# An estimate of engine times that orders a two-layer encoder program: its costs and slacks are changed

## The chip, the cores and the metric

The kernel runs on one core of one Trainium2 chip. The metric is the device time of one execution in microseconds; lower is better. The median of three executions before the change is 1813.26 us (1812.84 to 1814.89).

## The reference

A trunk of two residual layers over 512 tokens of width 1024, all in float32. Each layer adds half a gated feed-forward block, a mixer, and half a second feed-forward block to the residual stream; every part works on the root-mean-square norm of the stream:

```python
def _swiglu(h, w_gate, w_up, w_down):
    return (jax.nn.silu(h @ w_gate) * (h @ w_up)) @ w_down      # 1024 -> 2816 -> 1024

for layer in range(2):
    x = x + 0.5 * _swiglu(_rmsnorm(x, ...), ...)
    h = _rmsnorm(x, mix_norm[layer])
    if layer == 0:   # SSD heads (Mamba-2, chunks of 64) beside an S5 mixer (complex diagonal, 32 groups of 64 states)
        mixed = concat(ssd(h @ w[:, a]), s5(h @ w[:, b])) @ even_w_out
    else:            # chunked band attention beside a pooling mixer of four windows
        mixed = concat(attention(...), pool(...)) @ odd_w_out
    x = x + mixed
    x = x + 0.5 * _swiglu(_rmsnorm(x, ...), ...)
```

The S5 mixer needs tables that depend on its parameters only (powers of the discretised state matrix, input and output gains of 8 steps). The kernel works them out on the chip.

## The kernel before

**Stages.** Six stages run one after the other: f0 (first feed-forward), even (SSD and S5), f1, f2, odd (attention and pooling), f3. The residual stream lies transposed in eight tiles x of 128x512. A weight tile is loaded as float32 (raw, 512 KB), and split into a rounded part, copied by ScalarE (ACT), and a rest, taken by VectorE (DVE), both in tile whl. A product is then three matmuls (high by high, high by low, low by high), each 128x512, accumulated in a bank of PSUM (tile ps). Most of each feed-forward stage works on 256 columns with a scheme that needs seven block products for eight ("pairs"); the first tiles of it are done in the plain way ("classical"). In f0 the plain way reaches to q = 9 of 11, since the S5 tables are prepared beside it.

**Order.** Each engine runs its instructions in program order, and that order comes from a small simulation in the builder. `Builder` walks the main matmuls in a fixed order; after every group of three it calls `tick`, which moves on a set of generators ("threads", sorted by `PRIO`): the feed of split weights, evacuations of PSUM (`evac`), gates, norms, S5 and SSD pieces, attention blocks and the preparation of the S5 tables (`s5_prepare`). A generator says what it needs with `yield from self.on(engine, tiles)`, and goes on when the estimate says that this is there. `Clock` keeps the estimate: a time for each engine, and for each 64 elements of each tile the time of the last write and read. `Clock.cost` gives an instruction's duration, `Clock.note` moves the times. "Now" is the estimated time of TensorE (PE). So the estimate costs nothing at run time; it decides only which instruction stands ahead of which in each engine's order. What the chip waits for are semaphores that follow from the data.

**What `on` asks.** For PE a thread goes on when its inputs were ready `SLACK[stage]` before now (1.5 us in f0, 0.0 in even, 0.4 in odd). For ACT and DVE it goes on when inputs are ready within 0.3 us and the engine's estimated backlog is under `BACKLOG[stage]` (2.5 us in f0 and even, 3.0 in odd). With `ps=1` it also asks `side` for a bank of PSUM.

**Banks.** Eight banks lie in two pools of four, "b" for projection tiles, "a" for the down projections. `side` lets side work have a bank of "b" while fewer than `sideb` (2) are open, and else one of "a"; a bank counts as free from the estimated time of its last reader. `side_ps` asks `side` again and takes the bank.

**Table products.** In `s5_prepare`, `gains_of_outputs(e)` (eight times, two in flight) makes g1 on DVE, multiplies it by bmx in eight matmuls on PE (in the profile ps<-g,s5bm), copies the result to kt on ACT and writes it to HBM (prm). `gains_of_inputs(e)` (eight times, one in flight) makes bt on DVE, transposes it on PE (ps<-ident,bt), copies it to bl and writes it. The stage even reads prm.

**S5 in even.** `s5_bounce` writes u to HBM (s5us) and reads it back in 16 DMAs with runs of 64 elements into tile hg; `s5_eighth` multiplies that with the tables.

All compute instructions go through `Engine.call`, so nearly every row of the profile has its line, L205; tiles tell the rows apart.

Of the kernel before, what the change touches and what calls it, by code (L numbers as in the profile page):

```python
# [8 lines left out]
F32 = mybir.dt.float32  # L9
# [5 lines left out]
PSUM = bass.MemoryType.PSUM  # L15
DRAM = bass.MemoryType.DRAM

P = 128
S = 512
# [13 lines left out]
for _i, _pools in enumerate(((),(3,),(2,),(1,0))):  # L33
# [19 lines left out]
LAG = 4  # L53
WARM = 12
SLACK = {"f0": 1.5, "even": 0.0, "f1": 0.0, "f2": 0.0, "odd": 0.4, "f3": 0.0}
PRIO = {"evac": 0, "gate": 0, "small": 5, "prep": 6, "blocks": 6, "s5_bounce": 1, "s5_quarter": 0, "s5_gate": 0, "s5_eighth": 1,
        "ssd_dt": 1, "conv": 1, "ssd_chunk": 1, "ssd_tail": 0, "z": 2, "qk_norm": 0, "pool": 3, "attn": 2}
LIVE = 3
# [50 lines left out]
class Clock:  # L109


    def __init__(self):
        self.t = dict.fromkeys(list(ENGINES.values()) + ["RING", "DMA"], 0.0)
        self.t["ACT"], self.t["RING"], self.t["DVE"], self.t["PE"] = 1.9, 0.65, 0.6, 0.95
        self.w, self.r, self.floor, self.stuck = {}, {}, 0.0, 0
        self.lanes, self.born = [0.0] * 8, {}

    @property
    def now(self):
# [22 lines left out]
    @staticmethod  # L142
    def cost(eng, op, out, kw):
        n = max(out.free_size(), kw["in_"].free_size() if op == "tensor_reduce" else 0)
        if eng == "PE":
            if op == "transpose":
                return 0.12
            if kw["lhsT"].dtype == F32R:
                return max(0.11, 0.0025 + n / 2400)
            if out.partition_size() == 64:  # L150
                return 0.035 + n * 0.00084
            return max(0.21, 0.04 + n * 0.00168) if n < 512 else 0.86
        if eng == "ACT":
            return (0.2 if hasattr(kw.get("scale"), "space") or hasattr(kw.get("bias"), "space") else 0.09) + n * 0.00084
        one = op in ("tensor_scalar", "tensor_copy") and kw.get("in0", kw.get("in_")).space != PSUM
        ptr = any(hasattr(kw.get(k), "space") for k in ("scalar", "scalar1"))
        return (0.128 if ptr else 0.068) + n / (1920 if one else 960) * (1 if eng == "DVE" else 2)

    def note(self, eng, op, args, kw):
        out = kw.get("out", args[0] if args else None)  # L160
        outs = [out] + ([kw["accum_out"]] if "accum_out" in kw else [])
        ins = [v for k, v in kw.items() if k not in ("out", "accum_out") and hasattr(v, "free_size")]
        dma = op == "dma_start"
        at = self.t["RING"] if dma else self.t[eng]
        for ap in ins:
            for b in self.blocks(ap):
                t, e = self.w.get(b, (0.0, ""))
                at = max(at, t + (0.15 if e != eng else 0.11 if eng != "PE" else 0.0))
        for ap in outs:
            at = max(at, self.born.get(ap.name, 0.0))  # L170
            for b in self.blocks(ap):
                t, e = self.w.get(b, (0.0, ""))
                at = max(at, 0.0 if dma and e == "DMA" else t if e == eng else t + 0.1, self.r.get(b, 0.0))
        if dma and eng == "POOL":
            self.t["POOL"] = max(at, self.t["POOL"]) + 1.1
            end = max(self.t["DMA"], self.t["POOL"] + 1.0) + max(0.18, out.free_size() * out.partition_size() * 4 / 360e3)
            self.t["DMA"] = end
            end += 0.95
        elif dma:
            at = max(at, self.lanes.pop(0))  # L180
            self.t["RING"] = at + 0.48
            end = max(self.t["DMA"], at + 1.1) + max(0.06, out.free_size() * out.partition_size() * 4 / 360e3)
            self.t["DMA"] = end
            end += 1.06
            self.lanes.append(end)
        else:
            end = at + self.cost(eng, op, out, kw)
            self.t[eng] = end
        for ap in outs:
            for b in self.blocks(ap):  # L190
                self.w[b] = (max(end, self.w.get(b, (0.0, ""))[0]), "DMA" if dma else eng)
        for ap in ins:
            for b in self.blocks(ap):
                self.r[b] = max(self.r.get(b, 0.0), end)
# [55 lines left out]
class Builder:  # L250
# [44 lines left out]

    def add(self, kind, gen):
        p = PRIO[kind]
        i = next((i for i, (q, _) in enumerate(self.threads) if q >= p), len(self.threads))
        self.threads.insert(i, (p, gen))

    def idle(self):
# [13 lines left out]
            self.idle()  # L315


    def on(self, eng, *aps, ps=0):
        c = self.clk
        while True:  # L320
            r = c.ready(*aps)
            if eng == "PE":
                ok = r + SLACK[self.name] <= c.now
            elif eng == "DMA":
                ok = r <= c.now + 0.5
            else:
                ok = r <= c.now + 0.3 and c.t[eng] <= c.now + self.backlog
            if ok and (not ps or self.side(ps) is not None):
                return
            yield  # L330

# [22 lines left out]
            self.ring_of.pop(t.name).give(t)  # L354


    def side(self, n=1):
        which = None
        for w, most in (("b", self.sideb), ("a", 4)):
            ok = min(most - self.open[w], sum(t <= self.clk.now for t in self.freed[w]))  # L360
            if ok > 0:
                which = w
                n -= ok
        return which if n <= 0 else None
# [473 lines left out]
    def evac(self, ps, t, tag, m, done):  # L838
        while not self.scaled():
            yield  # L840
        if t[tag] is None:
            yield from self.room(tag, 1)
            if t[tag] is None:
                t[tag] = self.ft.tile([P, 2, S], F32, tag=tag, name=self.n(tag), bufs=1)
            else:
                self.leave(tag)
        yield from self.on("DVE", ps, self.rsB)
        self.evac_rs(ps, t[tag][:, m])
        self.free(ps)
        done.append(1)  # L850
# [84 lines left out]
    def pair(self, w, tag):  # L935
# [11 lines left out]
        self.nc.scalar.copy(out=p1, in_=X[:, hi])  # L947
        dst = self.ftile(tag)
        add(dst[:, 0, lo], X[:, lo], p1)
        self.free(X)  # L950
        Y = self.main_ps()
        a = self.block(Y[:, lo], W3, 0, TA, lo)
        self.block(Y[:, hi], W3, 512, TA, hi, a)
        self.give(W3)
        add(u2, Y[:, hi], p1)
        add(dst[:, 0, hi], Y[:, lo], u2)
        Z = self.main_ps()
        a = self.block(Z[:, lo], W4, 512, N[4:8], hi)
# [86 lines left out]
    def s5_prepare(self, pool):  # L1045
# [57 lines left out]
        for j in range(8):  # L1103
            n = 7 - j
# [26 lines left out]
        bmx, t16, t17 = tl("s5bm", [G + 1, 16]), tl("s5t16", [G, 16]), tl("s5t17", [G, 16])  # L1131
# [29 lines left out]
        def gains_of_outputs(e):  # L1161
# [3 lines left out]
            g1 = pool.tile([P, 4, 9, 16], F32, tag="s5g1", bufs=2, name=self.n("g1"))  # L1165
# [8 lines left out]
            nc.sync.dma_start(out=part(1), in_=g1[:, :, 1:9].rearrange("p g j i -> p g (j i)"))  # L1174
            yield from self.on("DVE")

            yield from self.on("PE", g1, bmx, ps=1)
            psk = self.side_ps()
            for i in range(4):
                nc.tensor.matmul(out=psk[32 * i:32 * i + 32, 0:P],  # L1180
# [20 lines left out]
        def gains_of_inputs(e):  # L1201
            gs = slice(4 * e, 4 * e + 4)
            prm = self.prm[e]
            part = lambda n: prm[:, 512 * n:512 * n + 512].rearrange("p (g c) -> p g c", g=4)
            bt = pool.tile([P, 4, 8, 16], F32, tag="s5bt", name=self.n("bt"))
            sh = [P, 4, 8, 16]
            v.tensor_tensor(out=bt, in0=brr[:, gs].unsqueeze(2).to_broadcast(sh),
                            in1=x1[:, gs].unsqueeze(3).to_broadcast(sh), op=ALU.mult)
            tb = pool.tile([P, 4, 8, 16], F32, tag="s5tc", name=self.n("tc"))
            v.tensor_tensor(out=tb, in0=bri[:, gs].unsqueeze(2).to_broadcast(sh),  # L1210
                            in1=x2[:, gs].unsqueeze(3).to_broadcast(sh), op=ALU.mult)
            v.tensor_tensor(out=bt, in0=bt, in1=tb, op=ALU.add)
            yield from self.on("PE", bt, ps=1)
            pst = self.side_ps()
            for i in range(4):
                nc.tensor.transpose(out=pst[:, i * P:(i + 1) * P], in_=bt[:, i].rearrange("p j i -> p (j i)"),
                                    identity=self.ident)
            bcal = pool.tile([P, 512], F32, tag="s5bl", bufs=2, name=self.n("bl"))
            yield from self.on("ACT", pst)
            nc.scalar.copy(out=bcal, in_=pst)  # L1220
            self.free(pst)
            yield from self.on("DMA", bcal)
            nc.sync.dma_start(out=prm[:, 0:512], in_=bcal)
            yield from self.on("DVE")
# [866 lines left out]
```

## Time and profile before

| | |
|---|---|
| median of three executions | 1813.26 us |
| the profiled execution | 1810.71 us, span 1808.7 us from first to last instruction |
| PE busy | 1792.4 us (99% of the span), 10514 matmuls |
| PE weight loads | 1564.3 us (86%) |
| DVE busy | 1428.9 us (79%), 2599 instructions |
| ACT busy | 754.7 us (42%), 1082 instructions |
| DMA | 207.16 MB, mean 115 GB/s |
| granted TensorE clock | 0.999 of full speed |

Busy time of PE counts a matmul up to its modelled end, and matmuls overlap; a distance between the starts of two matmuls says more of its rate than the busy time. Idle time of other engines costs nothing while PE has work. In rows of the timeline the first number is the start, the second the length, both in us; the bracket is the idle time ahead of it and what ended it.

### The profile page before, as it was taken

What the parts mean: (1) busy time and instruction counts of PE and PEld (TensorE: products, weight loads), DVE (VectorE), ACT (ScalarE), POOL (GpSimd) and SP (SyncE); (2) the same over time, 40 slices, a digit from 0 to 9 for tenths busy, and PEclk for the clock granted to TensorE, in tenths of its full rate; (3) what the DMA queues carried; (4) which work ended last, traced back from release to release, by engine and by line L of the source; (5) the groups of instructions that cost most, each with busy time, mean ns of one, the idle gap of its engine ahead of it and who ended that gap; (6) DMA issues with size and microseconds to landing.
All of it is one profiled execution on the core that took longest, in us unless ns stands there. A gap on an engine that the chain in (4) does not pass through costs nothing.

```text
span 1808.7 us, 26795 instructions
## 1 busy us (share of the span) xinstructions
PE 1792.4 (99%) x10514; PEld 1564.3 (86%) x10514; DVE 1428.9 (79%) x2599; ACT 754.7 (42%) x1082; POOL 18.7 (1%) x35
## 2 busy tenths in 40 slices
PE   9999999999999999999999999999999999999999
PEld 7877888978878889999988999998888788999997
DVE  8989877878986878887777988775578678988864
ACT  4323423433574444343343444333466544434331
POOL 0000000000010000000000000000000000000000
PEclk9999999999999999999999999999999999999999
DMA  5247432337773223332422333332434422333331
GB/s 196 92 141 190 144 103 82 117 130 205 201 168 114 88 89 104 118 105 95 138 64 78 106 117 97 103 102 86 144 78 111 129 82 76 100 106 107 111 98 70
DMA packets 80749, 207.16 MB, mean 115 GB/s; under 512 B 18000, under 2 KB 30320, under 8 KB 79472
## 3 DMA queue, kind: packets, MB, share of 16 engines
q1 hardware_dynamic: 78032, 196.52, 34.6%
q0 software_dynamic: 2448, 8.91, 3.1%
q8 instruction: 83, 1.36, 0.3%
q14 instruction: 42, 0.34, 0.1%
q10 hardware_dynamic: 144, 0.02, 0.0%
HBM read 192.82 MB, written 12.60 MB: 114 GB/s over the span
## 4 chain that ended last, share of the span: by engine, by line
PE 88%; DVE 8%; DMA 2%; issue 1%; ACT 1%; SPq 0%; DVEq 0%; ACTq 0%
PE ps L205 88%; DVE whl L205 1%; DVE hg L205 1%; DVE us L205 1%; DVE ex L205 1%; DVE ssb L205 1%; DMA raw<-in_wglu_dram 0%; DMA prm<-prm 0%; DMA s5ys<-ys 0%; ACT whl L205 0%; DVE s5x L205 0%; DMA ssb<-acsd 0%; DVE sc L205 0%; ACT hg L205 0%; DMA raw<-in_wgu_dram 0%
## 5 line engine op out<-in xcount | busy, mean ns | idle before, releaser
L205 PE MATMUL ps<-hg,whl 128*128 128x512 f32 (+1 forms) x8688 | 1609.6, 345 | 5.5 <-DVE hg L205 2.5
L205 PEld LDWEIGHTS ps<-hg,whl 128*128 128x128 f32 x8688 | 1375.5, 190 | 203.8 <-issue 4.6
L205 ACT CAST whl<-raw 128x1024 fp32r<-128x1024 f32 x366 | 383.0, 1051 | 532.3 <-PE ps L205 323.4
L205 DVE TENSOR_TENSOR whl<-raw,whl 128x1024 fp32r<-128x1024 f32 x349 | 424.1, 1222 | 180.8 <-ACT whl L205 180.3
L205 DVE SCALAR_TENSOR_TENSOR x<-ps,x 128x512 f32<-128x512 f32 x128 | 87.1, 688 | 37.0 <-PE ps L205 35.4
L205 DVE TENSOR_TENSOR raw<-raw,raw 128x512 f32<-128x512 f32 (+1 forms) x182 | 111.3, 649 | 2.2
L205 ACT CAST hg<-us 128x512 fp32r<-128x512 f32 x88 | 52.1, 620 | 105.2 <-DVE us L205 104.9
L205 PE MATMUL ps<-hg,wh 128*128 128x256 f32 x624 | 83.4, 283 | 0.0
L205 ACT ACTIVATE gs<-gs 128x1024 f32<-128x1024 f32 x44 | 46.7, 1060 | 85.5 <-DVE gs L205 85.5
L205 PEld LDWEIGHTS ps<-hg,wh 128*128 128x128 f32 x624 | 78.6, 192 | 0.0
L205 DVE TENSOR_TENSOR raw<-raw 128x512 f32<-128x512 f32 (+1 forms) x78 | 46.6, 597 | 16.4 <-DMA raw<-in_wgu_dram 16.4
L205 ACT COPY p<-ps 128x256 f32<-128x256 f32 x52 | 19.3, 372 | 95.5 <-PE ps L205 86.1
L205 DVE TENSOR_TENSOR hg<-us,hg 128x512 fp32r<-128x512 f32 x88 | 57.9, 685 | 0.0
L205 DVE TENSOR_TENSOR us<-gs,us 128x1024 f32<-128x1024 f32 x44 | 53.6, 1219 | 0.4
L205 ACT ACTIVATE hg<-x,gains 128x512 fp32r<-128x512 f32 x48 | 33.6, 722 | 32.4 <-DVE x L205 30.0
L205 ACT CAST hg<-raw 128x512 fp32r<-128x512 f32 x58 | 34.4, 622 | 21.3 <-DVE raw L205 20.6
L205 DVE TENSOR_TENSOR hg<-raw,hg 128x512 fp32r<-128x512 f32 x58 | 38.1, 689 | 0.1
L205 DVE SCALAR_TENSOR_TENSOR hg<-x,gains,hg 128x512 fp32r<-128x512 f32 x48 | 34.9, 746 | 2.5 <-ACT hg L205 2.5
L205 DVE TENSOR_TENSOR wh<-raw,wh 128x512 fp32r<-128x512 f32 x52 | 35.7, 686 | 0.0
L205 DVE TENSOR_TENSOR us<-ps,rsB 128x512 f32<-128x512 f32 x40 | 28.9, 723 | 4.5 <-PE ps L205 4.4
L205 ACT CAST wh<-raw 128x512 fp32r<-128x512 f32 x52 | 32.0, 616 | 0.0
L205 DVE TENSOR_TENSOR acc<-acc,sq 128x512 f32<-128x512 f32 x42 | 29.0, 690 | 0.9
(264 smaller groups left out, 1100.0 us busy)
## 6 DMA issues: line engine op xcount, KB each, us to landing
raw<-in_wgu_dram SPq DMA_DIRECT2D x176, 512.0 KB, 3.6
raw<-in_wdn_dram SPq DMA_DIRECT2D x88, 512.0 KB, 3.6
raw<-in_wev_dram SPq DMA_DIRECT2D x16, 512.0 KB, 3.6
prm<-prm SPq DMA_DIRECT2D x8, 1024.0 KB, 6.9
raw<-in_wod_dram SPq DMA_DIRECT2D x12, 512.0 KB, 3.6
raw<-in_wevo_dram SPq DMA_DIRECT2D x8, 512.0 KB, 6.6
raw<-in_wodo_dram SPq DMA_DIRECT2D x8, 512.0 KB, 6.4
x<-in_xT_dram SPq DMA_DIRECT2D x8, 256.0 KB, 5.6
```

Of the source, the lines that this page charges most:

```text
L205: r = f(*args, **kw)
```

## The change

It changes costs in `Clock`, the order of equal threads, and the slack of two places; no instruction is added or removed by it, other than what follows from another order.

- `Clock.cost`: a split matmul takes (n + 32) / 2400 us instead of max(0.11, 0.0025 + n / 2400): 0.2267 instead of 0.2158 for 512 columns, 0.120 instead of 0.110 for 256. A reciprocal takes 0.07 + n x 0.0062.
- `Clock.moved`: a DVE instruction takes 0.09 us more where its first partition, in quarters of 32, differs from that of the last read or write in the same memory.
- `Clock.short`: a DMA whose contiguous runs are under 128 elements, with at least 256 runs, lands 2.0 us later. By the shapes these are the 16 reads of s5us alone.
- `add`: an evac goes behind the threads of its priority, no longer ahead of them.
- `evac` reserves its tile in another way.
- `side` takes a slack: a bank must have been free that long. `on` hands its slack to it.
- The two kinds of table products ask for `PREP_SLACK` (3.0 us) instead of 1.5.

```diff
+PREP_SLACK = 3.0
...
+        self.reads, self.writes = {}, {}
...
             if kw["lhsT"].dtype == F32R:
-                return max(0.11, 0.0025 + n / 2400)
+                return (n + 32) / 2400
...
+        if op == "reciprocal":
+            return 0.07 + n * 0.0062
         return (0.128 if ptr else 0.068) + n / (1920 if one else 960) * (1 if eng == "DVE" else 2)
+
+    def moved(self, ins, out):
+        at = lambda ap: (ap.space == PSUM, ap.start_partition() // 32)
+        held = any(self.reads.get(m, q) != q for m, q in map(at, ins))
+        m, q = at(out)
+        held = held or self.writes.get(m, q) != q
+        self.writes[m] = q
+        for m, q in map(at, ins[::-1]):
+            self.reads[m] = q
+        return 0.09 if held else 0.0
+
+    @staticmethod
+    def short(aps):
+        def run(ap):
+            n = 1
+            for st, m in list(ap.ap)[:0:-1]:
+                if st != n:
+                    break
+                n *= m
+            return n
+        r = min(map(run, aps))
+        return 2.0 if r < 128 and aps[0].free_size() * aps[0].partition_size() >= 256 * r else 0.0
...
-            end += 1.06
+            end += 1.06 + self.short([out] + ins)
...
             end = at + self.cost(eng, op, out, kw)
+            if eng == "DVE":
+                end += self.moved([ap for ap in ins if ap.free_size() > 1], out)
...
     def add(self, kind, gen):
         p = PRIO[kind]
-        i = next((i for i, (q, _) in enumerate(self.threads) if q >= p), len(self.threads))
+        i = next((i for i, (q, _) in enumerate(self.threads) if q > p or q == p and kind != "evac"), len(self.threads))
...
-    def on(self, eng, *aps, ps=0):
+    def on(self, eng, *aps, ps=0, slack=None):
         c = self.clk
+        slack = SLACK[self.name] if slack is None else slack
...
-                ok = r + SLACK[self.name] <= c.now
+                ok = r + slack <= c.now
...
-            if ok and (not ps or self.side(ps) is not None):
+            if ok and (not ps or self.side(ps, slack) is not None):
...
-    def side(self, n=1):
+    def side(self, n=1, slack=0.0):
...
-            ok = min(most - self.open[w], sum(t <= self.clk.now for t in self.freed[w]))
+            ok = min(most - self.open[w], sum(t + slack <= self.clk.now for t in self.freed[w]))
...
     def evac(self, ps, t, tag, m, done):
         while not self.scaled():
             yield
+        while t[tag] is None and self.cnt.get(tag, 0):
+            yield
         if t[tag] is None:
-            yield from self.room(tag, 1)
-            if t[tag] is None:
-                t[tag] = self.ft.tile([P, 2, S], F32, tag=tag, name=self.n(tag), bufs=1)
-            else:
-                self.leave(tag)
+            self.cnt[tag] = 1
+            t[tag] = self.ft.tile([P, 2, S], F32, tag=tag, name=self.n(tag), bufs=1)
...
-            yield from self.on("PE", g1, bmx, ps=1)
+            yield from self.on("PE", g1, bmx, ps=1, slack=PREP_SLACK)
...
-            yield from self.on("PE", bt, ps=1)
+            yield from self.on("PE", bt, ps=1, slack=PREP_SLACK)
```

## The prediction, as put on record

> **What bounds the kernel now.** I read the page first (busy shares and the chain that ended last), then stretches, then who PE waited for, then the worst wait in the timeline.
>
> ```profile
> span 1808.7 us, 26795 instructions
> PE 1792.4 (99%) x10514; PEld 1564.3 (86%) x10514; DVE 1428.9 (79%) x2599; ACT 754.7 (42%) x1082; POOL 18.7 (1%) x35
> PE 88%; DVE 8%; DMA 2%; issue 1%; ACT 1%; SPq 0%; DVEq 0%; ACTq 0%
> ```
>
> PE is busy for all but 16.3 us of the span, and 88% of the chain is PE. The change adds and removes no matmul, so what it can win is PE's idle time and matmuls that ran slowly. The next rows say in which stages that lies, and the list of waits what it is (engine and tile that waited, what for, total, times, longest).
>
> ```profile
> 20.00:100.00 80.00, 78.36 (x361) 64.53 (x360) 76.23 (x266) 23.57 (x31) 0.00 (x0) 1.00 0.32 99
> 600.00:700.00 100.00, 100.00 (x596) 89.52 (x595) 88.18 (x136) 46.30 (x62) 0.00 (x0) 1.00 0.27 91
> ...
> PE ps L205 <- DVE hg L205: 3.0, 3, 1.5
> PE ps L205 <- DVE us L205: 2.9, 1, 2.9
> PE ps L205 <- DVE ones L205: 1.1, 1, 1.1
> PE ps L205 <- DVE whl L205: 1.1, 2, 0.5
> PE ps L205 <- DMA hg<-s5us: 0.8, 1, 0.8
> ...
> PE ps L205 <- DVE cr L205: 0.2, 1, 0.2
> ```
>
> The stretches are: length, then busy us of PE, PEld, DVE, ACT and POOL with their counts, granted clock, DMA share, GB/s. From 600 to 700 us, inside a later feed-forward stage, PE is busy 100.00 of 100: such stretches have nothing to win. The eleven rows of waits (first five and the last are shown) sum to 11.6 us in 14 waits. 2.7 us of that are at the start (ones, whl twice by DVE and 0.5 by ACT). The largest single one is 2.9 us, a table product in f0:
>
> ```profile
> 97.40 0.96 PE L205 MATMUL ps<-hg,whl 128*128 128x512 f32 x3
> 101.22 0.42 PE L205 MATMUL ps<-g,s5bm 128*32 128x128 f32 x8 [2.86 <-DVE us L205]
> ...
> 97.94 0.76 DVE L205 TENSOR_TENSOR g<-g,tb 128x576 f32<-128x576 f32 x1
> 98.62 1.22 DVE L205 TENSOR_TENSOR whl<-raw,whl 128x1024 fp32r<-128x1024 f32 x1
> 100.47 0.69 DVE L205 TENSOR_TENSOR us<-ps,rsB 128x512 f32<-128x512 f32 x1
> ...
> 98.00:101.00 3.00, 0.36 (x2) 0.00 (x0) 2.97 (x4) 0.67 (x3) 0.00 (x0) 1.00 0.76 248
> 101.00:106.00 5.00, 4.78 (x20) 3.71 (x21) 4.73 (x23) 2.08 (x5) 0.00 (x0) 0.66 0.47 161
> ```
>
> PE finished at 98.36 and reached the product. Its input g was done at 98.70, but the bank it was given was read by the evacuation us<-ps only until 101.16. DVE was full (2.97 of 3.00): the estimate had it further on than it was. Behind the stall the granted clock, the number before the DMA share, falls to 0.66 over 5 us, so the stall also costs 5.00 x (1 - 0.66) = 1.70 us. This one place is 2.86 + 1.70 = 4.56 us.
>
> **The change part by part.**
>
> *PE steps.* Two stretches of one kind of matmul give the real step:
>
> ```profile
> 267.69 19.65 PE L205 MATMUL ps<-hg,whl 128*128 128x512 f32 x85
> 1649.77 6.16 PE L205 MATMUL ps<-hg,whl 128*128 128x256 f32 x50
> L205 PE MATMUL ps<-hg,whl 128*128 128x512 f32 x4944 | 1158.8, 392 | 5.5 <-DVE hg L205 2.5 <-DVE whl L205 1.1 <-DVE pu L205 0.7
> L205 PE MATMUL ps<-hg,whl 128*128 128x256 f32 x3744 | 457.4, 283 | 0.0
> ```
>
> The last matmul's own length taken off, (19.65 - 0.392) / 84 = 0.229 us and (6.16 - 0.283) / 49 = 0.120 us. The old figures (0.2158, 0.110) are 6% and 8% short, the new ones (0.2267, 0.120) fit. So estimated PE time now runs faster per matmul: between 20 and 98 us some 350 matmuls by 0.0109 us are 3.8 us. Taken alone this makes side work look ready after fewer matmuls, which is earlier in PE's order, so it eats margin. [...]
>
> *DVE's small operations.* The table preparation copies between halves of the partitions:
>
> ```profile
> 59.06 0.18 DVE L205 COPY s5x<-s5pr 64x32 f32<-64x32 f32 x1
> 63.79 0.20 DVE L205 COPY s5x<-s5pr 64x32 f32<-64x32 f32 x1
> ...
> 88.89 0.20 DVE L205 COPY s5erp<-s5er 64x96 f32<-64x96 f32 x1
> 89.00 0.20 DVE L205 COPY s5eip<-s5ei 64x96 f32<-64x96 f32 x1
> 89.12 0.17 DVE L205 COPY s5m8p<-s5m 64x16 f32<-64x16 f32 x1
> 89.30 0.21 DVE L205 COPY s5erp<-s5er 64x96 f32<-64x96 f32 x1
> ...
> L205 DVE TENSOR_TENSOR s_sc<-s_t,s_t 64x128 f32<-64x128 f32 x32 | 9.2, 287 | 0.7
> ```
>
> From 59.06 to 63.79 there are 24 such copies that alternate halves, 4.73 / 23 = 0.206 us each, where the old formula gives 0.068 + 32 / 1920 = 0.085 and the new one 0.175. Copies within a half stand 0.11 and 0.12 apart, the one that changes it 0.18. Before 98 us some 41 instructions get 0.09 (32 of s5x, 4 of a1 and a2, 2 of bmx, 3 of erp and its like): 3.7 us, and the reciprocal 0.17, together 3.9 us of DVE time that the estimate lacked. In even 32 operations on s_sc get 2.9 us.
>
> *Table products later.* 1.5 us more slack. Shift against DVE at the stall: 1.5 + 3.9 - 3.8 = 1.6 us later than before. The slack on the bank helps less than it seems: `on` asks with 3.0, but `side_ps` asks again with 0.0, and in order "b", "a". At 98 us no down projection runs (its first weight was only loaded then), so "a" passes the question and "b" may be taken. I count only 1.6 us: the stall goes from 2.86 to 1.26. Bounds: 0 (the bank's slack does act, 3.0 > 2.86) to 2.86 (nothing). Does the clock fall after 1.26 us?
>
> ```profile
> 99.87 0.33 SPq L205 DMA_DIRECT2D raw<-in_wdn_dram  x1
> 537.57 2.79 PE L205 MATMUL ps<-hg,whl 128*128 128x512 f32 x11 [1.47 <-DVE hg L205]
> 520.00:540.00 20.00, 18.53 (x111) 14.75 (x110) 18.36 (x39) 15.05 (x20) 2.53 (x3) 1.00 0.61 141
> ```
>
> A wait of 1.47 us left it at 1.00, so the 1.70 us go whole. Term: -1.60 - 1.70 = -3.30 us.
>
> [...]
>
> *Tables done later.* The products of the inputs run one after the other, eight of them, those of the outputs two at a time, four rounds; with at most 3.0 us for each of the eight that is 24 us. Before even nothing reads the tables, but the preparation for the pairs (DVE work on raw and hg) starts when they are done.
>
> ```profile
> L205 SPq DMA_DIRECT2D prm<-kt x64: 302/424/1215, 125.3 to 196.2; - x64
> 250.00:270.00 20.00, 20.00 (x90) 16.56 (x89) 7.38 (x9) 5.26 (x6) 0.00 (x0) 1.00 0.36 106
> 270.00:290.00 20.00, 19.77 (x87) 15.80 (x86) 12.14 (x16) 5.27 (x6) 0.00 (x0) 1.00 0.18 52
> ```
>
> The last table DMA is issued at 196.2 and would move to 220 at worst. DVE has (20 - 7.38) + (20 - 12.14) = 20.5 us free before the pairs begin near 290. So this costs nothing while the delay stays under that; with the cover gone, 24 - 20.5 = 3.5 us of PE idle. I take 0.
>
> *Short transfers.* The reads of s5us are estimated to land 2.0 us later.
>
> ```profile
> 417.74 1.62 PE L205 MATMUL ps<-hg,prm 128*64 128x64 f32 x48 [0.77 <-DMA hg<-s5us]
> DMA to landing us min/median/max: 2.0/4.2/7.4
> ```
>
> The median read took 4.2 us; the old estimate was 1.1 + 0.06 + 1.06 = 2.2 us, the new one 4.2. PE waited 0.77 us for one; asked 2.0 us later, it does main matmuls meanwhile. Term -0.77 us. From the other side: S5 could start up to 2.0 us later in each of its two halves, 4.0 us, and the main order waits for its tiles later (the 3.0 us on hg). I take the gain, since what PE waited for was the landing itself, which doesn't move. The reads keep their place in SP's queue unless an estimate ahead of them moves; loads of weights behind them are asked for by room in their ring, and PE has no wait on a raw transfer in the list.
>
> *Evacuations in order, and the reservation.* A swap of two neighbours frees a bank one DVE operation earlier or later, 0.69 us by the row at 100.47; the projections have four banks in turn, so PE has another one meanwhile. 0, between -0.7 and +0.7 us. Without a free bank it would be one such operation for each tile.
>
> *Margin in even and odd*, where the slack is 0.0 and 0.4. By the code some 114 pieces of side work enter PE's order there (eight S5 and eight SSD pieces at two places each, tails and steps 6, attention 16 x 4, the rest 12). What PE's steps eat is 5% of what DVE is allowed to lag, 2.5 us: 0.125 us at each, 14 us if none had margin. But only some 8 of the 14 waits lie there, so nearly all have margin, and the 0.09 us on DVE act the other way (2.9 us in even). 0, between -1.1 (8 x 0.14) and +14 us.
>
> **Sum.** -3.30 - 0.77 = -4.07 us. The profiled execution took 1810.71 us (span 1808.7), 2.55 us under the median of 1813.26; it would go to 1806.6, the median to 1809.2 us. No change means within 0.2%, 3.6 us: 1809.6 to 1816.9, about what a measurement of this kernel can tell from no change. So the forecast stands just on the fast side of that.
>
> **The rivals.**
>
> 1. *More waits go than the one.* With DVE's time right, those of even and odd on hg, pu, prm and s could go as well: all but the start's are 11.6 - 2.7 = 8.9 us, with the clock 10.6, so 1802.7 us. For it: the waits are on DVE mostly, whose time was short. Against it: the two longest on hg after 500 us are main matmuls that wait for the mixers' results, which no estimate makes sooner.
> 2. *It doesn't do what it says.* The product is later, but takes a bank whose reader is late again, or another of the 16 products does. The shift of 1.6 us is less than the 2.86 us that it is late by, and the bank's slack is lost where "a" is free. 2.86 and 1.70 stay or come back elsewhere: 1812.5 us with the short transfer's gain.
> 3. *The clock's loss is not the stall's*: the clock falls there for another reason, and only 1.60 + 0.77 us come, 1810.9 us. Against it: the clock is 1.00 in all other stretches shown, with PE idle for less. [...]
> 4. *Slower: side work enters PE too early in even and odd.* PE's steps are 5% longer in the estimate, the slack there is 0.0 and 0.4. For it: it holds for each of 114 pieces, and PE waits in order. It decides when it costs over (4.07 + 3.63) / 114 = 0.068 us at each; at the full 0.125 us it is +14 - 4.1, so 1823 us, at 0.09 some 1819. Against it: so few of them wait now.
>
> **How the numbers follow.** Forecast 0.42 (its own range 1806 to 1811; about 0.30 of it faster, 0.12 within 0.2%), rival 1 0.20, rival 2 0.15, rival 3 0.06, rival 4 0.15, late pairs 0.02. Faster: 0.30 + 0.20 = 0.50. Same: 0.12 + 0.15 + 0.06 = 0.33. Slower: 0.17. The range goes from 1802.5, all of rival 1, to 1817, where rival 4 begins: it leaves out most of rival 4 and a little of rival 1, under 2 in 10. Predicted is the forecast, 1809.2 us.
>
> **What would show it.** Right: the wait of ps<-g,s5bm on DVE under 1.5 us or gone, the granted clock 1.00 between 100 and 110 us; no wait on hg<-s5us; the last prm<-kt between 196 and 220 us and PE busy 19.7 of 20 or more near 290. Wrong: a wait of over 2.5 us at another product with the clock down behind it (rival 2); a clock that falls without a wait (rival 3); more than some 20 waits of PE, in even and odd, on DVE's s, ps readers or ssb (rival 4). What would make it wrong altogether is that another order of the same work is no better placed by true times than by wrong ones, for the places the estimate still misses.

## The result, and the profile after

The change makes the kernel slower: 1827.56 us (median of 5 runs, 1825.67 to 1829.22) against 1813.26 us (5 runs, 1811.10 to 1814.89) for the kernel before, a ratio of 1.0083 with a 95% interval of 1.0072 to 1.0095. The prediction was 1809.2 us. The profiled execution of after took 1825.67 us. The loss is 14.3 us in the medians and 15.3 us in the spans of the two profiled executions.

The page of after (busy time by engine, and the chain that ended last):

```profile
span 1824.0 us, 26797 instructions
PE 1797.3 (99%) x10514; PEld 1565.8 (86%) x10514; DVE 1429.8 (78%) x2600; ACT 757.9 (42%) x1084; POOL 18.6 (1%) x35
PE 85%; DVE 9%; issue 3%; DMA 2%; ACT 1%; SPq 0%; DVEq 0%; ACTq 0%; POOLq 0%
```

The busy share of 99% doesn't show the loss: PE waits for 26.7 us instead of 16.3, and its busy time, in which the same matmuls ran, is 4.9 us longer. The last write of x in each stage marks its end: f0 ends at 382.7 us (before 382.5), even takes 212.5 us (before 197.0), f1 and f2 348.4 each (348.2 and 348.5), odd 180.7 (181.6). So one stage holds the whole loss. The same stretch of before, and then stretches of after, as length, busy us of PE, PEld, DVE, ACT and POOL, granted clock, DMA share, GB/s:

```profile
382.50:579.50 197.00, 192.19 (x1124) 156.20 (x1123) 158.93 (x385) 98.80 (x164) 7.79 (x9) 1.00 0.65 181
```

```profile
20.00:100.00 80.00, 79.84 (x362) 66.03 (x361) 76.03 (x266) 23.42 (x28) 0.00 (x0) 1.00 0.31 98
...
382.70:595.20 212.50, 196.73 (x1123) 159.49 (x1122) 159.26 (x385) 100.98 (x166) 7.77 (x9) 0.95 0.59 168
600.00:700.00 100.00, 100.00 (x541) 86.85 (x540) 85.87 (x140) 41.93 (x54) 0.00 (x0) 1.00 0.24 82
270.00:290.00 20.00, 18.63 (x82) 14.85 (x81) 12.11 (x17) 5.25 (x6) 0.00 (x0) 1.00 0.16 52
```

From 20 to 100 us the change does what it was to do: PE is busy 79.84 of 80 (before 78.36) and the wait at 98 us is gone. In even PE does the same work in 15.5 us more, at a mean clock of 0.95. Who PE waited for, over the whole program of after (total, times, longest):

```profile
PE ps L235 <- DMA whl<-in_wev_dram: 5.3, 1, 5.3
PE ps L235 <- DMA prm<-prm: 4.9, 1, 4.9
PE ps L235 <- ACT whl L235: 3.0, 1, 3.0
PE ps L235 <- DVE bt L235: 1.7, 1, 1.7
PE ps L235 <- DVE x L235: 1.4, 1, 1.4
```

L235 is in after what L205 is in before, the helper's line. The first three rows are in even. In before the first was not in the list, prm had 0.6 us and ScalarE's whl 0.5 (at the start of the program). A wait on hg<-s5us is no longer in the list. The places in the timeline of after, and then two stretches behind them:

```profile
427.84 0.39 PE L235 MATMUL ps<-s_sc,prm 128*128 128x63 f32 x2
428.25 0.33 SPq L235 DMA_DIRECT2D prm<-prm  x1
...
433.15 1.12 PE L235 MATMUL ps<-hg,prm 128*64 128x64 f32 x16 [4.93 <-DMA prm<-prm]
...
493.48 1.04 ACT L235 ACTIVATE whl<-raw 128x1024 fp32r<-128x1024 f32 x1
...
494.85 0.99 POOL L235 DMA_DIRECT2D whl<-in_wev_dram  x1 [493.16 <-ACT whl L235]
...
495.51 1.22 PE L235 MATMUL ps<-hg,whl 128*128 128x512 f32 x2 [2.98 <-ACT whl L235]
...
502.07 0.80 PE L235 MATMUL ps<-hg,whl 128*128 128x512 f32 x1 [5.33 <-DMA whl<-in_wev_dram]
```

```profile
433.00:436.00 3.00, 2.85 (x22) 2.48 (x22) 1.62 (x5) 0.00 (x0) 0.00 (x0) 0.50 0.67 238
...
505.00:508.00 3.00, 3.00 (x8) 2.36 (x8) 2.04 (x5) 0.82 (x1) 0.84 (x1) 0.50 0.74 115
```

Read them in order. PE's last product of one S5 eighth, at 427.84, frees a buffer of prm; only then, at 428.25, can SyncE issue the load of a later eighth into it, and PE's next instruction is the product that needs this load. The load lands 4.8 us later and PE stands. In before the load into that buffer is issued on the same event, at 429.33, and lands after 4.9 us; there PE has other work in its order meanwhile. So it isn't the load that became slower. Later a weight is split by way of a transfer: ScalarE writes the negated copy at 493.48, GpSimd's DMA adds the weight onto it from 494.85, and ScalarE writes the rounded part. PE waits 2.98 us for ScalarE's part, and two matmuls later 5.33 us for the transfer. That transfer lands 7.2 us after its issue, and the first of its kind in before took 7.2 us too; but there it was issued 25 us sooner, and PE didn't wait for it:

```profile
469.82 1.00 POOL L205 DMA_DIRECT2D whl<-in_wev_dram  x1 [468.13 <-ACT whl L205]
```

In after the split stands in ScalarE's order behind a run of S5 and SSD pieces, which keep ScalarE busy for 13.2 of the 13.4 us from 480.10 to 493.48. Behind both places the granted clock is 0.50. The waits of even sum to 15.6 us against 4.6 before, +11.0; the other 4.5 of the 15.5 us are longer busy time, with the clock at 0.50 behind these waits.

### The profile page after: what moved, and what is told of

Its sections match the earlier page's. It is cut to its first block, busy times and chain, and to the rows that moved or that the text cites. A ratio compares the mean times of both kernels' runs of the same rounds, so it can differ in the third digit from the quotient of the medians.

```text
span 1824.0 us, 26797 instructions
## 1 busy us (share of the span) xinstructions
PE 1797.3 (99%) x10514; PEld 1565.8 (86%) x10514; DVE 1429.8 (78%) x2600; ACT 757.9 (42%) x1084; POOL 18.6 (1%) x35
## 4 chain that ended last, share of the span: by engine, by line
PE 85%; DVE 9%; issue 3%; DMA 2%; ACT 1%; SPq 0%; DVEq 0%; ACTq 0%; POOLq 0%
PE ps L235 85%; DVE whl L235 2%; DVE us L235 1%; DVE hg L235 1%; DVE ct L235 1%; DVE ex L235 1%; DMA whl<-in_wev_dram 0%; ACT whl L235 0%; DVE bt L235 0%; DVE s5x L235 0%; DVE x L235 0%; DVE gs L235 0%; SPq L235 0%; DVE sc L235 0%; DMA prm<-bl 0%
## 5 line engine op out<-in xcount | busy, mean ns | idle before, releaser
L235 PE MATMUL ps<-hg,whl 128*128 128x512 f32 (+1 forms) x8688 | 1612.8, 345 | 11.3 <-DMA whl<-in_wev_dram 5.3
L235 PEld LDWEIGHTS ps<-hg,whl 128*128 128x128 f32 x8688 | 1375.8, 190 | 209.9 <-DMA whl<-in_wev_dram 6.1
L235 ACT CAST whl<-raw 128x1024 fp32r<-128x1024 f32 x366 | 383.1, 1049 | 549.2 <-PE ps L235 339.3
L235 DVE TENSOR_TENSOR whl<-raw,whl 128x1024 fp32r<-128x1024 f32 x349 | 425.0, 1222 | 206.8 <-ACT whl L235 206.2
L235 DVE SCALAR_TENSOR_TENSOR x<-ps,x 128x512 f32<-128x512 f32 x128 | 86.4, 687 | 37.7 <-PE ps L235 36.1
L235 DVE TENSOR_TENSOR raw<-raw,raw 128x512 f32<-128x512 f32 (+1 forms) x182 | 110.7, 649 | 1.9
L235 ACT CAST hg<-us 128x512 fp32r<-128x512 f32 x88 | 51.5, 617 | 95.0 <-DVE us L235 95.0
L235 PE MATMUL ps<-hg,wh 128*128 128x256 f32 x624 | 83.4, 283 | 0.0
L235 PEld LDWEIGHTS ps<-hg,wh 128*128 128x128 f32 x624 | 78.6, 192 | 0.0
L235 ACT ACTIVATE gs<-gs 128x1024 f32<-128x1024 f32 x44 | 46.6, 1059 | 58.9 <-DVE gs L235 58.9
L235 DVE TENSOR_TENSOR hg<-us,hg 128x512 fp32r<-128x512 f32 x88 | 58.0, 685 | 0.0
L235 DVE TENSOR_TENSOR raw<-raw 128x512 f32<-128x512 f32 (+1 forms) x78 | 46.6, 597 | 11.4 <-DMA raw<-in_wgu_dram 11.2
L235 DVE TENSOR_TENSOR us<-gs,us 128x1024 f32<-128x1024 f32 x44 | 53.7, 1220 | 0.4
L235 ACT CAST hg<-raw 128x512 fp32r<-128x512 f32 x58 | 34.2, 619 | 45.7 <-DVE raw L235 45.3
L235 ACT COPY p<-ps 128x256 f32<-128x256 f32 x52 | 19.3, 370 | 77.1 <-PE ps L235 77.1
L235 ACT ACTIVATE hg<-x,gains 128x512 fp32r<-128x512 f32 x48 | 33.7, 720 | 41.6 <-DVE x L235 39.3
L235 DVE TENSOR_TENSOR hg<-raw,hg 128x512 fp32r<-128x512 f32 x58 | 38.0, 689 | 0.3
L235 DVE SCALAR_TENSOR_TENSOR hg<-x,gains,hg 128x512 fp32r<-128x512 f32 x48 | 35.5, 746 | 3.5 <-ACT hg L235 3.5
L235 DVE TENSOR_TENSOR wh<-raw,wh 128x512 fp32r<-128x512 f32 x52 | 35.6, 685 | 0.0
L235 ACT CAST wh<-raw 128x512 fp32r<-128x512 f32 x52 | 32.1, 617 | 0.0
L235 DVE TENSOR_TENSOR us<-ps,rsB 128x512 f32<-128x512 f32 x40 | 28.8, 720 | 1.0 <-PE ps L235 0.9
L235 DVE TENSOR_TENSOR acc<-acc,sq 128x512 f32<-128x512 f32 x42 | 28.8, 686 | 0.8
```

What stands on the lines that cost most here:

```text
L235: r = f(*args, **kw)
```

## The experiments

Two words for what follows. A *side piece* is an instruction of PE in even that is no main matmul, 282 of them; how far it stands from its place in before is counted in main matmuls ahead of it, from the orders of the two programs. In the order of after 250 of them have moved, by 14.7 main matmuls earlier on average. *Mend* means that the estimate is told of something that it lacked. Each length of a stage is that of one profiled execution; the times are medians.

**e1, the change with the old step of PE; e2, before with the new step alone.**

```diff
-                return (n + 32) / 2400
+                return max(0.11, 0.0025 + n / 2400)      # e1, in after; e2 the reverse, in before
```

> The kernel after with the old step of PE in the estimate (0.2158 us for 512 columns, 0.110 for 256); all else of the change stays. Theory 1 (the longer step takes away a margin that covered transfers in even): even goes back from 212.5 to 197 us within 2, the two waits of 4.9 us on the prm load and 5.3 us on the whl transfer go, and f0 keeps its gain, so 1808 to 1813 us. Theory 2 (the 2.0 us for short transfers holds S5 back): even stays over 207, the time over 1822. Theory 3 (any new order of even is a draw): even anywhere from 195 to 215, with other waits.

> The kernel before with the new step of PE alone. Theory 1: even is long here too, 207 us or more, with waits of over 4 us on transfers, and the stall of 2.86 us in f0 grows, since PE's estimate is now faster and DVE's is not: 1822 to 1832 us. Theory 2: even stays 197 within 2 and the time under 1817. Theory 3: anywhere.

e1: 1824.46 us, ratio 1.0063 (1.0048 to 1.0078), even 208.0. e2: 1825.51 us, 1.0066 (1.0050 to 1.0082), f0 ends 6.8 us later than before, even 205.6. Neither account fits alone: e1 falls where theory 2 had it (over 207), e2 near where theory 1 had it (207 or more). The new step costs 8.6 us in even by itself, but without it the rest of the change costs 11.0. The prm load makes PE wait 0.83 us in e1 and 2.49 in e2; e1 has other waits (2.90 us on hg, 2.62 on a wglu weight, 2.10 and 1.50 on ssb).

**e3, the last three wev weights split on DVE; e4, a transfer starts no earlier than now.**

```diff
-BY_DMA = {"wev": (13, 16), "wglu": (0, 2), ...
+BY_DMA = {"wglu": (0, 2), ...                            # e3
...
-            at = max(at, self.lanes.pop(0))
+            at = max(at, self.lanes.pop(0), self.now)    # e4
```

> The kernel after with the last three wev weights split by ScalarE and VectorE like the others, not by a transfer that adds onto the negated copy. Theory 1: the waits of 2.98 and 5.33 us on whl near 500 us go, and the clock behind them comes back, 8 to 11 us less: 1816 to 1820; the 4.9 us wait on the prm load stays. If the time stays over 1824, the weights came late for another reason than the way of their split.

> The kernel after, with an estimate in which no transfer of SyncE starts before the moment at which it is issued (one line: its start is at least now). Theory 1: the wait of 4.93 us on the prm load near 428 us goes with the low clock behind it, 6 to 8 us less, 1819 to 1822; the two waits on whl near 500 us may stay. Theory 2 or 3: no change, or another pattern of waits.

e3: 1831.55 us, 1.0104 (1.0087 to 1.0121), even 214.2. The wait on whl<-in_wev_dram went, but of the one on ScalarE's whl 2.02 us stay (2.98 in after, at the same place), since ScalarE comes to the split no sooner, and a new one came, 3.53 us on ssb; my forecast of 1816 to 1820 was wrong. e4: 1818.86 us, 1.0033 (1.0022 to 1.0044), even 204.5. The longest waits of PE from the list of e3, and then from that of e4:

```profile
PE ps L235 <- DMA prm<-prm: 5.0, 1, 5.0
PE ps L235 <- DVE ssb L235: 3.5, 1, 3.5
```

```profile
PE ps L235 <- DVE ysq L235: 3.1, 2, 2.4
PE ps L235 <- DVE hg L235: 1.9, 1, 1.9
PE ps L235 <- DVE bt L235: 1.6, 1, 1.6
```

The first row of e4 is no transfer; neither the prm load nor the weight is in its list at all. So with one more line in the estimate the 4.93 us are gone (even is 8.0 us shorter, theory 1 had 6 to 8). This order is new as well, and the waits on whl went in it, which the line wasn't meant for; that the line itself did it is argued from the code: the estimate let a transfer start as soon as its queue was free, even if that lay before the moment of issue, and it knows nothing of the buffer's last reader; so it took the load for landed and let PE go on. But even is still 7.5 us longer than in before.

**e5 to e7, one part alone on before; e8, a neutral shift.**

```diff
+        yield from self.on("PE", g1, bmx, ps=1, slack=3.0)            # e5, also for bt, and the slack in side
+            end += 1.06 + self.short([out] + ins)                     # e6
+                end += self.moved(...)                                # e7, and the reciprocal's cost
-                return max(0.11, 0.0025 + n / 2400)
+                return max(0.11, 0.0037 + n / 2400)                   # e8
```

> The kernel before with the later table products alone (3.0 us for the two kinds, and the slack handed on to the question for a bank); all costs as before. PE's order in even is that of before, instruction for instruction. The prediction's step: the wait of 2.86 us on the evacuation at 98 us goes with the 0.66 clock behind it, even stays at 197 us within 1, so 1808 to 1810 us. Its rival 2 (the bank's reader is late again, or another product): the 2.86 us stay or come back in f0, 1812 to 1814 us.

> The kernel before with the 2.0 us for short transfers alone. The order in f0 is that of before; in even PE's order differs from the first S5 piece on. Theory 1 (the step of PE is what counts): the wait of 0.77 us on hg<-s5us goes, even 196 to 198 us, 1811 to 1814. Theory 2 (S5 is held back): even 199 to 203, since S5 starts 2 us later in each half. Theory 3 (before's order of even is a good draw, and every other order costs): even 201 to 212 with waits at new places, on transfers or on DVE, that have nothing to do with s5us.

> The kernel before with the costs of DVE alone (0.09 us for a change of partitions, and the reciprocal). The stall of 2.86 us in f0 should shrink, since DVE is estimated 3.9 us later there. Theory 1: even 197 within 2, since PE's step is as before, so 1808 to 1812 us. Theory 3: even 201 to 212 all the same, though these costs are right.

> The kernel before with a step of PE that is 0.0012 us longer per matmul in the estimate (0.0037 instead of 0.0025 beside n / 2400): a tenth of the change's step, no more right than before. Theory 1, by proportion: a ninth of the 15.5 us at most, even 197 to 199 us, 1812 to 1815. Theory 3: the order of even differs from before's after some 466 instructions of PE, and even takes 201 to 212 us.

| | us | ratio (95%) | f0 ends | even |
|---|---|---|---|---|
| e5 later products | 1812.31 | 0.9993 (0.9984 to 1.0003) | 382.7 | 198.6, order of before |
| e6 short transfers | 1817.44 | 1.0020 (1.0010 to 1.0029) | 380.9 | 203.3 |
| e7 small DVE costs | 1834.82 | 1.0114 (1.0099 to 1.0129) | 378.6 | 221.0 |
| e8 1.2 ns a matmul | 1822.29 | 1.0046 (1.0031 to 1.0061) | 382.9 | 203.0 |

e8 decides against theory 1 as it stood: a ninth of the change's step, no more right than the old one, costs 6.0 us of even, not 1.5. And e5 shows what became of the table product, in its timeline and the stretch behind:

```profile
100.76 0.69 DVE L205 TENSOR_TENSOR us<-ps,rsB 128x512 f32<-128x512 f32 x1
...
101.60 4.76 PE L205 MATMUL ps<-hg,whl 128*128 128x512 f32 x13 [2.25 <-DVE us L205]
```

```profile
101.00:106.00 5.00, 4.40 (x13) 3.55 (x14) 4.80 (x21) 0.00 (x0) 0.00 (x0) 0.69 0.55 173
```

The product is later, but the evacuation us<-ps ends at 101.5 us (in before at 101.2), and now it is a *main* product that waits for it. DVE was late, not the table product early. In e7, where the estimate knows DVE's small operations, table work on DVE itself is put off, and f0 is 3.9 us shorter.

e7's even is the longest of all, past the 212 us of theory 3. Its timeline on PE, then on ScalarE, then on DVE:

```profile
485.34 2.27 PE L233 MATMUL ps<-ssb 128*64 128x128 f32 x10 [4.74 <-DVE ssb L233]
509.67 0.79 PE L233 MATMUL ps<-hg,whl 128*128 128x512 f32 x1 [5.27 <-DMA whl<-in_wev_dram]
```

```profile
479.45 0.63 ACT L233 ACTIVATE g<-yv 128x512 f32<-128x512 f32 x1 [5.90 <-DMA yv<-s5ys]
498.59 0.63 ACT L233 ACTIVATE g<-yv 128x512 f32<-128x512 f32 x1 [7.29 <-DMA yv<-s5ys]
```

```profile
480.11 0.69 DVE L233 SCALAR_TENSOR_TENSOR g<-g,yv 128x512 f32<-128x512 f32 x1 [4.11 <-ACT g L233]
```

Three engines stand one behind the other: ScalarE has an S5 quarter's g<-yv at the head of its order and waits 5.90 us for the read of yv from HBM; DVE, in order too, waits 4.11 us for that g; the SSD chunk's ssb stands behind them on both, and PE waits 4.74 us for ssb. What looks like a late DVE is a late transfer two steps back. The read itself stands behind two weights, in the timeline of GpSimd and then of SyncE:

```profile
471.11 0.99 POOL L233 DMA_DIRECT2D whl<-in_wev_dram  x1 [469.43 <-DVE s_sc L233]
```

```profile
471.75 0.33 SPq L233 DMA_DIRECT2D raw<-in_wglu_dram  x1
472.30 0.32 SPq L233 DMA_DIRECT2D yv<-s5ys  x1
```

The weights land at 477.4 (raw) and 479.0 us (whl), and the read 0.4 us after the second, 7.1 us after its issue. The writes that it reads back had landed 2.5 us before it was issued. ScalarE's list in before has no wait on yv in even.

**e9, the costs of DVE in f0 alone.** The same as e7, if the stage is f0; even and odd keep the old costs, and PE's order in even is that of before.

```diff
+            fine = self.name == "f0"
-            end = at + self.cost(eng, op, out, kw)
+            end = at + self.cost(eng, op, out, kw, fine)
+            if eng == "DVE" and fine:
+                end += self.moved([ap for ap in ins if ap.free_size() > 1], out)
```

> The kernel before with the costs of DVE (0.09 us for a change of partitions, and the reciprocal) in stage f0 alone; the estimate of even and odd keeps the old costs, and PE's order in even is that of before again, instruction for instruction. Theory 3 (each new order of even costs; the estimate of f0 is a gain by itself): f0 378.6 us within 1 as with these costs everywhere, even 197 to 199, so 1808 to 1811 us. If even is long again although its order is that of before, theory 3 falls: then it is what f0 leaves behind that costs.

1808.85 us (1807.40 to 1811.15, 11 runs), ratio 0.9977 (0.9968 to 0.9986): faster than both kernels, and within theory 3's range on each count. f0 ends at 378.7, even takes 198.1. Its stretches:

```profile
100.00:110.00 10.00, 10.00 (x59) 7.60 (x58) 9.12 (x29) 4.45 (x11) 0.00 (x0) 1.00 0.53 173
...
378.70:576.80 198.10, 192.51 (x1124) 156.19 (x1123) 159.00 (x385) 98.86 (x164) 7.79 (x9) 1.00 0.64 180
```

**e10, e13 to e16: is it the margin?** A slack of 1.0 us in even (e10 in after, e13 in before), 2.0 us (e15), and neutral steps.

```diff
-SLACK = {"f0": 1.5, "even": 0.0, ...
+SLACK = {"f0": 1.5, "even": 1.0, ...          # e10 after, e13 before, e14; 2.0 in e15
-                return (n + 32) / 2400
+                return (n + 31) / 2400        # e14 with the slack, e16 without
```

> The kernel after with a slack of 1.0 us instead of 0.0 in even. In the order of after the side pieces of even stand 14.7 main matmuls earlier on average than before (250 of 282 instructions moved); with this slack they stand 5.8 later than before. Theory 1 (too early is what costs): no wait of over 2 us on a transfer is left in even, and even takes 200 us or less, the time 1809 to 1815. Theory 3 (any order other than before's costs): the transfer waits go, but others come, even 202 to 212, the time 1816 to 1826.

> The kernel before with a slack of 1.0 us in even, old costs. Side pieces of PE stand 11.0 main matmuls later on average than before (242 of 282 moved). Theory 1 (margin alone): no harm, even 196 to 200 us, the time 1811 to 1816. Theory 3 (any new order is a draw, before's was a good one; a slack doesn't mend costs that are wrong): even 201 to 212 with waits on DVE or transfers, the time 1816 to 1828.

> The kernel after with 1.0 us of slack in even and a neutral step of PE ((n + 31) / 2400, 0.0004 us less). 71 of 282 instructions of even stand elsewhere than in the run with the slack and the change's step. Theory 1 (right costs and a margin make the order good): even 198 to 202 us again. Theory 3: even over 203.

> The kernel after with 2.0 us of slack in even. Side pieces stand 9.9 main matmuls later than before. Theory 1: still no waits on transfers, and a little later at the end of the stage, where the main products wait for the mixers' results: even 199 to 203 us. Theory 3: anywhere from 198 to 212.

> The kernel after with the neutral step (n + 31) / 2400 and no slack in even, as in the change. Side pieces stand 5.9 main matmuls earlier than before (in the change 14.7). Theory 1, by proportion of the shift: even 202 to 207 us. Theory 3: anywhere from 200 to 221, with another set of waits than the change's.

e10 came out at 1811.75 us (0.9995, 0.9986 to 1.0004), even 200.2, and seemed to settle it for the margin. It didn't hold: e14, 0.4 ns a matmul away from e10, took 1825.78 us (1.0072, even 204.8, f0 3.9 us longer than in before), e15 1823.34 us (1.0059, even 210.1), e13 1829.22 us (1.0090, even 213.6), e16 1834.57 us (1.0116, even 212.1, f0 and odd 6.7 and 4.8 us longer). In e15 the chain of e7 is back, with the read of yv again right behind two weights: ScalarE waits 7.88 us for yv, DVE 7.47 for ScalarE, and PE 6.59:

```profile
513.92 0.48 PE L235 MATMUL ps<-ssb,H 128*64 128x128 f32 x2 [6.59 <-DVE H L235]
```

What goes with a slack or the mend is the long wait on the prm load. Where the change stood with its new step (or the neutral one), no slack and no mend, it was 4.93, 4.99 and 5.08 us (after, e3, e16); with a slack or the mend it was at most 0.81 us, in all eight (e4, e10 to e12, e14, e15, e17, e18). Without the change the picture is weaker: 2.49 us in e2, 1.08 in e13 with its slack, and at most 0.63 in the other orders that have neither.

**e11, e12, e17, e18: the mended estimate.** Four mends in after: transfers as in e4; a prm load waits for the last reader of its buffer; a transfer that adds onto a tile lands 3.0 us later; a change of ScalarE's table costs 1.28 us, and the way of a silu is chosen when it is issued. e12 and e18 with 1.0 us of slack in even, e17 and e18 with a neutral step.

```diff
+            at = max(at, self.lanes.pop(0), self.now)
+            self.clk.born[t.name] = self.clk.used(self.slots[-1 - LIVE])   # prm buffers
-            end += 0.95
+            end += 3.95                                                     # GpSimd's transfers
+            end = at + self.cost(eng, op, out, kw) + self.table(eng, kw)    # 1.28 at Exp <-> Silu
```

> The kernel after with four mends in the estimate: no transfer starts before now; a prm load waits for the last reader of its buffer; a transfer that adds onto a tile lands 3.0 us later; ScalarE's change of tables costs 1.28 us, and the choice between the two ways of a silu is made when it is issued, so that only one change of tables is left in even. Theory 4 (what costs is what the estimate still lacks, and with it every order is good): even 200 us or less, no wait of PE over 2 us there. Theory 3: waits at new places on DVE, even 201 to 212.

> The same mends and a slack of 1.0 us in even. Theory 4: even 195 to 200, as short as before's or shorter, the time 1808 to 1813. Theory 3: even over 201.

> The mended estimate without slack and with a neutral step, (n + 31) / 2400; 116 of 282 instructions of even stand elsewhere than in the mended run. Theory 4 (what the estimate lacks is what costs): no wait on the prm load over 1 us, even 205 us or less. Theory 3 (any order is a draw): even anywhere from 200 to 220.

> The mended estimate with 1.0 us of slack in even and a neutral step, (n + 33) / 2400; 96 of 282 instructions stand elsewhere than in the mended run with that slack. Theory 4: even 197 to 203 us. Theory 3: anywhere from 198 to 215.

e11 1816.47 us (1.0022, 1.0013 to 1.0031), e12 1811.39 (0.9996, 0.9986 to 1.0005), e17 1827.14 (1.0079, 1.0063 to 1.0096), e18 1812.31 (0.9997, 0.9988 to 1.0007; its profiled execution is the slowest of its ten, 1817.75). All orders of even that ran, in us:

| | no slack | slack |
|---|---|---|
| order of before | 197.0, 198.6 (e5), 198.1 (e9) | |
| new orders, no mend, old step | 203.0 (e8), 203.3 (e6), 208.0 (e1), 221.0 (e7) | 213.6 (e13) |
| new orders, no mend, new step | 205.6 (e2), 212.5 (after), 214.2 (e3), 212.1 (e16) | 200.2 (e10), 204.8 (e14), 210.1 (e15) |
| mended (e4: one mend of four) | 204.5 (e4), 202.2 (e11), 207.1 (e17) | 198.9 (e12), 196.9 (e18) |

So each new order without a mend is a draw between 200 and 221, and the order of before, whose three executions differ by 1.6 us, lies below all of them. What makes that order good was not found. Only mends and slack together came as low, in two orders of two, which differ in 96 of 282 side pieces. Two are few: whether that is a class or two more good draws stays open. The mends alone don't do it: e11 missed theory 4's 200 us, with waits of 2.80 and 2.23 us left, and e17 its 205 (3.75 us on whl<-in_wev_dram again).

## Why the prediction was wrong, by its own steps

- **Margin in even and odd** is the step that failed. It stood in the sum with 0, between -1.1 and +14 us, on the ground that only some 8 of the 14 waits of before lie there, "so nearly all have margin". In after even took 15.5 us more (odd 0.9 less), past the upper bound of that term. The waits of before tell of before's order. They say nothing of another order, in which other pieces stand next to what is late. e8 moved 100 of the 282 pieces by a shift without meaning and lost 6.0 us.
- **Rival 4 came nearest**, with another mechanism. It (chance 0.15, 1817 to 1823 us) had the sign and the stage, too early side work in even; its highest price is 9.9 us, and 14.3 were measured. It looked for more than 20 waits, on DVE, at 0.125 us a piece. There were six in even, and 13.2 of their 15.6 us were three that the prm load and one weight's split made. The rule by proportion doesn't hold either: a ninth of the step cost 6.0 us (e8), the whole step alone 8.6 (e2).
- **Table products later**, -1.60: nothing by itself. e5 shifts the wait from the product to a main product (2.86 to 2.25 us, clock 0.69). Rival 2 foresaw that 2.86 and 1.70 stay or come back elsewhere, and so it was in e5. That e5's 1812.31 is near rival 2's 1812.5 is chance: that sum has 0.77 us of the short transfers in it, which e5 lacks.
- **DVE's small operations** were sized right in the estimate (3.9 us that it lacked) and put in the sum only as part of the shift at one product. Alone they gave 3.9 and 3.8 us of f0 (e7, e9), more than the whole of that term: the table product's wait is gone there, and so is the low clock behind it. In after f0 gains nothing (382.7): waits of 1.67 us on bt and 1.37 on x stand in place of the old one. In e1, with the old step, f0 has one of 2.61 us and ends at 382.1, so f0's gain is missing without the step too; what loses it, the later products, the order of the evacuations or the mixture, was not told apart.
- **The clock**, -1.70: it came back at 98 us (1.00 from 100 to 110). The low clock stood behind 26 of the 28 waits of 2.49 us or more in all traces, not behind each, see below; rival 3 (the loss is not the stall's) is made less likely by that and not ruled out.
- **Short transfers**, -0.77: the wait went in after, e1 and e6. What the estimate's later landing does to the order of even cost 6.3 us in e6, where I had allowed 4.0.
- **Tables done later**: the last prm<-kt was to move to between 196 and 220; it is issued at 188.0. PE from 270 to 290 is busy 18.63 of 20, under the 19.7 asked for; the rest is the one wait of 1.37 us on x.
- The last sentence on what would make it wrong altogether, that another order is no better placed for the places the estimate still misses, is what happened. It had no price in the sum, and that is the same gap as in the first point: e8, whose step is no truer than the old one, shows it.

## What to carry to other kernels

When a change alters the inputs of a planner, price it as a new draw of the whole order, not as a shift of the places that you can see: take two or three neutral shifts of an input first, and their spread is the range. An order that came out well can hide what the planner doesn't know; look there first for transfers (here PE waited 4.93 us for one that was issued late because a buffer was in use, and 5.33 for one that added onto a tile, and ScalarE 5.90 for one read back from HBM behind a weight), and follow a wait through the engines that run in order until one waits for something that isn't an engine. A better cost did no harm where it left the sensitive stage's order alone, as in e9.

## What the runs showed of the hardware

The same wait was not always followed by the low clock. In e6 the order of f0 is that of before, and the same product waits as long:

```profile
101.20 0.43 PE L228 MATMUL ps<-g,s5bm 128*32 128x128 f32 x8 [2.85 <-DVE us L228]
```

```profile
101.00:106.00 5.00, 4.80 (x27) 3.83 (x28) 4.73 (x23) 1.98 (x5) 0.00 (x0) 1.00 0.50 161
```

The clock is 1.00 where before had 0.66, and f0 ends 1.6 us earlier (380.9), about the 1.70 us of the prediction. e13 has the order of before in f0 too, and there the same wait (2.85 us) is followed by the low clock, as in before: its last two products ps<-hg,wdt start at 385.99 us, in before at 386.19, in e6 at 384.63. Why the clock stayed up in e6 was not shown.

Over the 20 traces there are 28 waits of PE of 2.49 us or more. The granted clock stands at 0.50 behind 26 of them; the other two are this one of e6 and the one of 2.49 us in e2. Of the 46 waits of 1.5 to 2.48 us 18 were followed by it. In before it falls at 101.58 us, 0.36 us after the end of the wait, and stands at 0.50 for 3.41 us; in after it falls 1.58 us into the wait of 4.93 us, for 6.83 us, and 2.13 us into the wait of 2.98 us, for 13.65 us. In the 3.41 us of before PE does eight matmuls of 512 columns, 0.43 us each where the prediction had measured 0.229: at 0.50 a loss of 3.41 x 0.50 = 1.7 us. And it fell three times (e2 at 1308, e16 at 1315, e18 at 1296 us) with no more than 0.27 us of waiting in the 7 us ahead, which is the sign that the prediction gave for rival 3.

ScalarE's table loads (1.28 us each) differ from order to order: one in even in before, three in after, e1, e3, e4, e13 and e15. The read of yv back from HBM landed between 2.6 and 10.8 us after its issue in these runs; the three behind the chains of e7 and e15 (6.7 to 7.3 us) landed within 1 us of a weight that was issued ahead of them.
